# The modulation vectors of a two-layer diffusion step: from GpSimd and VectorE to TensorE and a later stage

## The chip, the cores and the metric

The kernel runs on one core of a Trainium2 chip, as one launch. A core has TensorE (PE, matrix products; PEld is its weight load), VectorE (DVE), ScalarE (ACT), GpSimd (POOL) and SyncE (SP, which here only issues DMAs). The metric is the device time of one execution in microseconds (us); less is better.

## The reference

The reference is one step of a backbone of two layers over 1152 tokens (1024 latent, 128 context) of width 1024. What matters here are the modulation vectors. Each layer has six of them for each of two conditions (`c` for latent tokens, `c_ctx` for context tokens):

```python
def ada_mod(cvec, w, b):
    m = jnp.matmul(jax.nn.silu(cvec), w) + b      # cvec (1024,), w (1024, 6144)
    return jnp.split(m, 6, axis=-1)
...
    sh1, sc1, g1, sh2, sc2, g2 = ada_mod(c_ctx, w_mod[l], b_mod[l])
    u = rms_norm(xp, norm1_g[l]) * (1.0 + sc1) + sh1
    mix, ... = context_mixer(u, lp, lam_init)
    xp = xp + g1 * mix
    xp = xp + g2 * swiglu(rms_norm(xp, norm2_g[l]) * (1.0 + sc2) + sh2, w_gate_up[l], w_down[l])
```

The mixers behind the input projection are a differential attention (4 heads), a gated delta rule and an mLSTM (4 heads each, two directions, in chunks). All is fp32.

## The kernel before, in words

Activations lie transposed, features on the 128 partitions, tokens along the rows, in three groups of 384 tokens (`GW`). A dense product is split in two fp32r parts (`split`, `load_w`), so a 128x128 block of weights by 384 tokens is three matrix products (`mm3`, L187, with the lines L189, L190 and L191). `load_w` (L174) loads 512 KB of raw weights into a slot `wr` (two slots, issued by ACT's queue), ACT casts it to `wh` (L183) and VectorE subtracts for `wl` (L184); there are three slots each of `wh` and `wl`.

A layer runs: `begin` (the first token-major columns), `w_in` (the input projection and what the mixers need), `mixers` (scans and attention with the output projection), the norm and `ffn`. In `w_in`, after the gates (`gates1`), a loop of ten blocks (`blk_b` six times, `blk_c` four times) makes 128 columns each: 72 products of 384 columns; `blk_b` follows with a short convolution on VectorE (L704 to L708) and, for four of them, sums of squares by small fp32 matrix products of 2 columns (L715, nine in the code of a block). Then come the preparation of nine chunks (`prep1`, L730), the inverses (`inverse`), `prep2`, and the attention's columns (`blk_a`, `tok_cols`). PSUM has eight banks: here two for `dn` and six for `pp`.

The modulation has 48 blocks of 128 values a layer. The first 16 of layer 1 are made at the start (`adaln`). The others are the side work of the ten-block loop, written out in `run` (L1359): blocks 16 to 47 of the layer, and in layer 1 also blocks 0 to 15 of layer 2. From the second turn on the loop adds up to six blocks (layer 1) or four (layer 2). A block (`ada`, L231) is one DMA of 512 KB by SP's queue into one of five slots `aw`, the weights transposed; for the first condition VectorE multiplies by the SiLU of the condition and sums along the row in one instruction (L240); for the second GpSimd multiplies (L243) and ACT sums (L244). The condition's SiLU, on all partitions, is `csb` (`ada_open`, L225). The pool of these tiles lies where the tiles of `prep1` come later.

In `ffn` (L354) a hidden block `gu` takes two weights and two rows of products (`pg`, `pu`), and `dn` takes two hidden blocks and their two down weights (`pd`), which `add_gated` (L344) adds to the residual on VectorE (L347). The loop issues `gu(j + 2)`, `dn((j, j + 1))`, `gu(j + 3)`.

A planner that simulates the engines sets the order of the instructions on each queue: of those that are ready in its own clock it takes the one that stands first in the program, and a tile gets a slot of its ring in the same way. On the chip each queue then runs strictly in that order.

Of the kernel before, what the change touches and what calls it, by code (L numbers as in the profile page):

```python
# [45 lines left out]
AWB = 5  # L46
# [6 lines left out]
HS = (0, 2, 1, 3)  # place of each head in the stored chunk matrices  # L53

# column ranges of the small parameter array
# [15 lines left out]
class Kern:  # L71
# [24 lines left out]
    # ---------------------------------------------------------------- constants  # L96
    def setup(self, es):
# [3 lines left out]
        # silu(c) for both conditions, split in two parts, as the stationary operand of the modulation product  # L101
# [18 lines left out]
    def setup2(self):  # L120
# [4 lines left out]
        # fp32r operands of the decay matrices: identity, ones, and a large negative number where masked  # L125
# [15 lines left out]
    def setup3(self):  # L141
        nc = self.nc
        # lambda of the attention and exp(A_log)
# [29 lines left out]
    # ---------------------------------------------------------------- dense products  # L173
# [32 lines left out]
    # ---------------------------------------------------------------- modulation vectors  # L206
    def adaln(self, l, jbs, pool, psp, tag, bufs, raw=None):
        """Blocks of 512 columns jbs of silu(c) @ w_mod + b_mod, as per-partition columns."""
# [16 lines left out]
    def ada_open(self, pool):  # L225
        """silu(c) for both conditions, on every partition."""
        self.csb = self.t(pool, [P, 2, D], "csb", 1)
        self.nc.sync.dma_start(self.csb, self.A["cB"].to_broadcast([P, 2, D]))
        self.nc.scalar.activation(self.csb, self.csb, AF.Silu)  # L229

    def ada(self, l, b, pool, bufs, dve):  # L231
        """Block b of silu(c) @ w_mod, a column per condition: products summed along the rows of the transposed weights."""
        nc = self.nc
        w = self.t(pool, [P, D], "aw", bufs)
        nc.sync.dma_start(w, self.A["w_mod1"][b] if l else self.A["w_mod0"][b - 16])
        for i in range(2):
            o = self.mod[l][:, b, i:i + 1]
            if i in dve:
                j = self.t(pool, [P, D], "aj", 1)
                nc.vector.scalar_tensor_tensor(out=j, in0=w, scalar=1.0, in1=self.csb[:, i], op0=ALU.mult, op1=ALU.mult, accum_out=o)  # L240
                continue
            p = self.t(pool, [P, D], "ap", APB)
            nc.gpsimd.tensor_tensor(out=p, in0=w, in1=self.csb[:, i], op=ALU.mult)  # L243
            nc.scalar.activation(p, p, AF.Copy, accum_out=o)  # L244
# [26 lines left out]
    # ---------------------------------------------------------------- norms  # L271
# [3 lines left out]
    def stat(self, g, k, xt):  # L275
        """Adds the squares of block k of group g to the group's sum."""
# [9 lines left out]
    def stats(self, g, x, pool):  # L286
        """The squares of group g, added up in two parts."""
# [9 lines left out]
    def rstd(self, g, psp, tag="st", bufs=2, tag2=None):  # L297
        """1/rms of the tokens of group g, on every partition, in PSUM."""
# [17 lines left out]
    def norm_g(self, x, a, sh, g, R):  # L316
        """A generator over the blocks of group g."""
# [17 lines left out]
    def norm_y(self, x, g, R):  # L335
        """The final norm of group g."""
        nc = self.nc
        for k in range(KB):
            t = self.t(self.nw, [P, GW], "nt", 4)
            nc.vector.scalar_tensor_tensor(out=t, in0=x[g][k], scalar=self.p(0, "fg")[:, k:k + 1], in1=R, op0=ALU.mult, op1=ALU.mult)  # L340
            nc.sync.dma_start(self.O["y"][:, k, GW * g:GW * g + GW], t)
            yield
# [7 lines left out]
    # ---------------------------------------------------------------- FFN  # L350
# [3 lines left out]
    def ffn(self, l, x, u, hp, psp, before, norm):  # L354
# [27 lines left out]
        def dn(bs):  # L382
# [6 lines left out]
            # the last one by groups, with the norm that follows  # L389
# [15 lines left out]
        gu(1)  # L405
        for j in range(0, HB, 2):
            if j + 2 < HB:
                gu(j + 2)
            dn((j, j + 1))
# [4 lines left out]
    # ---------------------------------------------------------------- input projection and preparation of the mixers  # L414
    def open_s(self, l):
        """Places in DRAM for what passes from the projection to the mixers, and the banks of the projection."""
# [20 lines left out]
    def begin(self, l, u, norm):  # L437
        """The first columns of the projection, along with the norm of the last group."""
        with self.pool("first", side="right") as pr:
# [3 lines left out]
            u[2] = list(norm(2, self.rstd(2, self.pp, "pp", 6)))  # L443
# [3 lines left out]
    def w_in(self, l, u, side, ed, pe):  # L447
        nc, A, S = self.nc, self.A, self.S
        with ExitStack() as es:
# [6 lines left out]
            side = list(side)  # L456
            with self.pool("side", side="right") as sp:
                self.ada_open(sp)
                n = -(-len(side) // (10 - LATE))
                for b in range(10):  # L460
# [6 lines left out]
                    if b >= LATE:  # L467
                        for l1, jb in side[:n]:
                            self.ada(l1, jb, sp, AWB, (0,))
                        side = side[n:]  # L470
                self.ada_bias(l, 16, 48)
                self.ada_scale(l, self.a2[l], "n2g", 32)
                if l == 0:
                    self.ada_bias(1, 0, 16)
                    self.ada_scale(1, self.a1[1], "n1g", 8)
# [30 lines left out]
    def tok_cols(self, l, u, i, pr):  # L506
        """Token-major columns: i = 0: cv and gates, 1, 2: av, 3: bg, 4: co."""
# [16 lines left out]
        for tt in range(NCH):  # L524
            g, j = divmod(tt, 3)
            cs = slice(128 * j, 128 * j + 128)
            ps = self.ps(self.pp, "pp", 6) if i == 0 and 1 < tt < 8 else self.ps(self.dn, "dn", 2)
# [995 lines left out]
```

## Time and profile before

| what | value |
|---|---|
| three runs | 3964.11, 3953.47, 3959.14 us; median 3959.14 |
| span of the profiled execution | 3963.4 us, first to last instruction |
| PE, PEld busy | 3587.5, 3417.7 us |
| VectorE, ScalarE, GpSimd busy | 2333.4, 1223.3, 904.9 us |
| mean granted TensorE clock | 0.939 of full speed |

The profile is of an execution of its own; its device time is not listed apart from its span, which lies within the three runs' times. "Busy" counts instructions on the engine, not its queue's waits. The granted clock has two levels, 1.00 (2.4 GHz) and 0.50 (1.2 GHz); a value between is a mean over a stretch. A matrix product's duration overlaps that of the next, so the pace is read from starts or from counts in a stretch. An fp32 product (not fp32r) stands as two instructions in the trace.

### The profile page before, as it was taken

The numbers are of one execution on the slowest core, as the hardware profiler recorded it, in microseconds if no ns is written. First come the engines' busy times: TensorE is split into PE (matmuls) and PEld (weight loads), VectorE is DVE, ScalarE is ACT, GpSimd is POOL, SyncE is SP. The second block draws the span as 40 slices with busy tenths as digits, with TensorE's granted clock in tenths as the row PEclk, the third lists the DMA queues.
The fourth block names the chain that finished last, engine by engine and source line by source line (L and its number), as shares of the span: only waits on it lengthen the run. The fifth ranks groups of instructions, "written<-read, shape, count | busy, mean of one in ns | idle before, by whom it ended". The sixth has DMA issues, their size and how long they took to land. (4 is left out here: it accounts for less than half of the span.)

```text
span 3963.4 us, 59219 instructions
## 1 busy us (share of the span) xinstructions
PE 3587.5 (91%) x22770; PEld 3417.7 (86%) x22770; DVE 2333.4 (59%) x5009; ACT 1223.3 (31%) x2544; POOL 904.9 (23%) x983
## 2 busy tenths in 40 slices
PE   7876888888899999999988798988889999999998
PEld 6876777788789999999987777878779999999997
DVE  7898575768654333333378957656785533433335
ACT  5343322535533111111143442233463411111111
POOL 2276340246310000000023735013551200000001
PEclk8988997899899999999998899979999999999999
DMA  5355743485411111111133575248652111111111
GB/s 206 129 197 165 241 159 111 118 242 155 149 54 38 38 49 43 38 43 43 40 121 135 192 246 182 90 114 246 175 160 68 38 43 38 44 47 38 38 49 59
DMA packets 270177, 434.11 MB, mean 110 GB/s; under 512 B 23880, under 2 KB 185736, under 8 KB 269640
## 3 DMA queue, kind: packets, MB, share of 16 engines
q1 hardware_dynamic: 240664, 324.28, 26.1%
q10 hardware_dynamic: 29232, 106.05, 8.4%
q8 instruction: 180, 2.95, 0.3%
q14 instruction: 101, 0.83, 0.1%
HBM read 315.85 MB, written 114.39 MB: 109 GB/s over the span
## 5 line engine op out<-in xcount | busy, mean ns | idle before, releaser
L347 DVE SCALAR_TENSOR_TENSOR x<-pd,mod,x 128x256 f32<-128x256 f32 (+1 forms) x832 | 404.1, 513 | 667.9 <-PE pd L191 667.2
L183 ACT CAST wh<-wr 128x1024 fp32r<-128x1024 f32 (+1 forms) x219 | 228.6, 1045 | 831.2 <-PE pu L190 457.6
L284 POOL TENSOR_TENSOR nacc<-nacc,nsq 128x384 f32<-128x384 f32 x48 | 52.0, 1083 | 1758.0 <-ACT nsq L283 1750.8
L189 PE MATMUL dn<-uh,wh 128*128 128x384 f32 x864 | 312.9, 362 | 82.7 <-ACT gw L726 37.7
L184 DVE TENSOR_TENSOR wl<-wr,wh 128x1024 fp32r<-128x1024 f32 (+1 forms) x219 | 279.9, 1287 | 164.1 <-ACT wh L183 163.6
L189 PE MATMUL pd<-hh,wh 128*128 128x384 f32 x1056 | 359.6, 341 | 6.9 <-DVE x L347 5.1
L190 PE MATMUL pg<-ul,wh 128*128 128x384 f32 x1056 | 357.9, 339 | 1.8 <-DVE ul L332 1.8
L189 PE MATMUL pg<-uh,wh 128*128 128x384 f32 x1056 | 356.0, 337 | 2.6 <-ACT uh L327 2.6
L190 PE MATMUL pd<-hl,wh 128*128 128x384 f32 x1056 | 356.2, 337 | 0.0
L191 PE MATMUL pd<-hh,wl 128*128 128x384 f32 x1056 | 355.9, 337 | 0.0
L189 PE MATMUL pu<-uh,wh 128*128 128x384 f32 x1056 | 355.3, 336 | 0.0
L190 PE MATMUL pu<-ul,wh 128*128 128x384 f32 x1056 | 355.3, 336 | 0.0
L191 PE MATMUL pg<-uh,wl 128*128 128x384 f32 x1056 | 353.1, 337 | 0.0
L191 PE MATMUL pu<-uh,wl 128*128 128x384 f32 x1056 | 349.1, 336 | 0.0
L190 PE MATMUL dn<-ul,wh 128*128 128x384 f32 x864 | 309.2, 358 | 0.0
L191 PE MATMUL dn<-uh,wl 128*128 128x384 f32 x864 | 307.8, 356 | 0.1
L243 POOL TENSOR_TENSOR ap<-aw,csb 128x1024 f32<-128x1024 f32 x80 | 253.2, 3191 | 220.9 <-ACT csb L229 147.0
L1232 PE MATMUL s<-K,Q 128*128 128x384 f32 (+1 forms) x800 | 229.1, 397 | 57.3 <-DMA Q<-QD 28.8
L189 PEld LDWEIGHTS dn<-uh,wh 128*128 128x128 f32 x864 | 175.1, 203 | 95.1 <-ACT gw L726 39.6
L1233 DVE TENSOR_SCALAR_CACHE_REDUCE e<-s 128x384 f32<-128x384 f32 (+1 forms) x400 | 209.8, 540 | 78.8 <-PE s L1232 73.2
L370 DVE TENSOR_TENSOR hs<-pu,hs 128x384 f32<-128x384 f32 x132 | 73.1, 554 | 239.8 <-PE pu L191 238.2
L189 PEld LDWEIGHTS pd<-hh,wh 128*128 128x128 f32 x1056 | 198.1, 188 | 15.8 <-issue 7.5
(354 smaller groups left out, 8650.3 us busy)
## 6 DMA issues: line engine op xcount, KB each, us to landing
wr<-in_w_gu_dram ACTq DMA_DIRECT2D x88, 512.0 KB
aw<-in_w_mod_dram SPq DMA_DIRECT2D x80, 512.0 KB
wr<-in_w_dn_dram ACTq DMA_DIRECT2D x44, 512.0 KB
wr<-in_w_st_dram ACTq DMA_DIRECT2D x36, 512.0 KB
rd<-RD SPq DMA_DIRECT2D x36, 512.0 KB
Q<-QD SPq DMA_DIRECT2D x64, 256.0 KB
RM<-em SPq DMA_DIRECT2D x36, 384.0 KB
rm<-RM SPq DMA_DIRECT2D x36, 384.0 KB
```

The costliest lines, as they stand in the source:

```text
L183: nc.scalar.copy(hi, r)
L184: (eng or nc.vector).tensor_tensor(out=lo, in0=r, in1=hi.bitcast(F32), op=ALU.subtract)
L189: mm(out, lhsT=wh, rhs=xh, start=start, stop=False)
L190: mm(out, lhsT=wh, rhs=xl, start=False, stop=False)
L191: mm(out, lhsT=wl, rhs=xh, start=False, stop=stop)
L243: nc.gpsimd.tensor_tensor(out=p, in0=w, in1=self.csb[:, i], op=ALU.mult)
L284: (nc.gpsimd if k in PST else nc.vector).tensor_tensor(out=self.acc[g], in0=self.acc[g], in1=s, op=ALU.add)
L347: nc.vector.scalar_tensor_tensor(out=x[g][k][:, lo:hi], in0=ps[:, lo:hi], scalar=gate[:, k, cnd:cnd + 1], in1=x[g][k][:, lo:hi], op0=ALU.m ...
L370: nc.vector.tensor_mul(s, pu[:, :GW], s)
L1232: nc.tensor.matmul(p[:, :w], lhsT=q[:, m, hl, 128 * j:128 * j + 128], rhs=K[m][:, 128 * ks[0]:128 * ks[0] + w], start=hl == 0, stop=hl == 1)
L1233: nc.vector.tensor_scalar(out=e[:, GW * i:GW * i + w], in0=p[:, :w], scalar1=0.125, scalar2=None, op0=ALU.mult, op1=ALU.max, accum_out=mx[ ...
```

## The change

Layer 1's blocks 16 to 47 become matrix products: the weights lie untransposed by blocks (`_blocks`), a block is eight fp32 products of 128x128 by the 2 columns of `cs`, all 32 blocks summing into one PSUM bank. The bank comes from `pp`, which has five instead of six everywhere. Layer 2's 48 blocks move into layer 1's `ffn`, five or six in each of nine turns, on VectorE alone, in three pieces of the row for each condition; the partial sums are added up once at j = 18. Their weights go into the two `wr` slots of the FFN's weights, loaded by SP's queue; the products' unused result goes into a bank of `st`; the SiLUs lie in free buffers of the norm's pool. GpSimd makes none. Layer 2's `w_in` has no side work. `tok_cols` uses `pp` for one token tile less; other edits take out comments.

```diff
-AWB = 5
+AWB = 4
+ACH = ((0, 384), (384, 768), (768, 1024))
...
+    def ada_pe(self, b, ps):
+        nc = self.nc
+        w = self.t(self.side, [P, D], "aw", AWB)
+        nc.sync.dma_start(w, self.A["w_mod0"][b - 16])
+        o = ps[:, 2 * (b - 16):2 * (b - 16) + 2]
+        for k in range(KB):
+            nc.tensor.matmul(o, lhsT=w[:, 128 * k:128 * k + 128], rhs=self.cs[:, k, :], start=k == 0, stop=k == KB - 1)
+
+    def ada_open(self):
+        nc = self.nc
+        self.apart = self.t(self.nw, [P, 48, 2, 3], "apart", 1)
+        self.csb = []
         for i in range(2):
+            for lo, hi in ACH:
+                t = self.t(self.nw, [P, GW], *(("nt", 4) if len(self.csb) < 4 else ("nacc", 3)))[:, :hi - lo]
+                nc.sync.dma_start(t, self.A["cB"][0, i:i + 1, lo:hi].to_broadcast([P, hi - lo]))
+                nc.scalar.activation(t, t, AF.Silu)
+                self.csb.append(t)
+
+    def ada(self, b, junk):
+        nc = self.nc
+        w = self.t(self.stage, [P, D], "wr", 2)
+        nc.sync.dma_start(w, self.A["w_mod1"][b])
+        for i in range(2):
+            for j, (lo, hi) in enumerate(ACH):
+                nc.vector.scalar_tensor_tensor(out=junk[:, :hi - lo], in0=w[:, lo:hi], scalar=1.0, in1=self.csb[3 * i + j],
+                                               op0=ALU.mult, op1=ALU.mult, accum_out=self.apart[:, b, i, j:j + 1])
+
+    def ada_close(self):
+        nc = self.nc
+        nc.vector.reduce_sum(self.mod[1].rearrange("p b i -> p (b i)"), self.apart.rearrange("p b i j -> p (b i) j"), axis=AX.X)
+        self.ada_bias(1, 0, 48)
+        self.ada_scale(1, self.a1[1], "n1g", 8)
+        self.ada_scale(1, self.a2[1], "n2g", 32)
...
         gu(1)
+        if l == 0:
+            self.ada_open()
+            junk = self.ps(psp, "st", 2)
         for j in range(0, HB, 2):
             if j + 2 < HB:
                 gu(j + 2)
+            if l == 0 and j < 20:
+                if j == 18:
+                    self.ada_close()
+                else:
+                    for b in range(16 * j // 6, 16 * (j + 2) // 6):
+                        self.ada(b, junk)
             dn((j, j + 1))
...
-            side = list(side)
-            with self.pool("side", side="right") as sp:
-                self.ada_open(sp)
-                n = -(-len(side) // (10 - LATE))
+            side = list(range(16, 48)) if l == 0 else []
+            with ExitStack() as ss:
+                if side:
+                    self.side = ss.enter_context(self.pool("side", side="right"))
+                    pm = self.ps(self.dn, "ad", 1)
...
-                    if b >= LATE:
-                        for l1, jb in side[:n]:
-                            self.ada(l1, jb, sp, AWB, (0,))
-                        side = side[n:]
-                self.ada_bias(l, 16, 48)
-                self.ada_scale(l, self.a2[l], "n2g", 32)
-                if l == 0:
-                    self.ada_bias(1, 0, 16)
-                    self.ada_scale(1, self.a1[1], "n1g", 8)
+                    for jb in side[4 * b:4 * b + 4]:
+                        self.ada_pe(jb, pm)
+                if side:
+                    m = self.mod[0][:, 16:48, :]
+                    nc.vector.tensor_add(m, pm[:, 0:64].rearrange("p (b i) -> p b i", i=2),
+                                         self.p(0, "bmod")[:, 16:48][:, :, None].to_broadcast([P, 32, 2]))
+                    self.ada_scale(0, self.a2[0], "n2g", 32)
...
-                ps = self.ps(pp, "pp", 6)
+                ps = self.ps(pp, "pp", 5)
...
-    out["w_mod0"] = x["w_mod"][0, :, 2048:].T.reshape(32, P, D)
+    out["w_mod0"] = _blocks(x["w_mod"][0, :, 2048:])
```

## Rows read from the trace of the kernel before

**Rows 1.** The profile's page, first part: busy time and share by engine.
```profile
PE 3587.5 (91%) x22770; PEld 3417.7 (86%) x22770; DVE 2333.4 (59%) x5009; ACT 1223.3 (31%) x2544; POOL 904.9 (23%) x983
```

**Rows 2.** Windows: stretch, length; PE, PEld, DVE, ACT, POOL busy (instructions); clock; DMA; GB/s.
```profile
2061.00:2264.00 203.00, 162.11 (x930) 157.70 (x930) 185.00 (x209) 82.79 (x135) 102.75 (x32) 0.87 0.47 157
...
1183.00:1933.00 750.00, 749.36 (x4306) 746.09 (x4305) 292.09 (x520) 136.07 (x222) 9.03 (x11) 1.00 0.13 41
```

**Rows 3.** Waits of PE in 2061:2264: total us, times, longest.
```profile
PE dn L189 <- ACT gw L726: 19.0, 2, 12.4
PE pp L715 <- ACT cv L712: 16.7, 1, 16.7
```

**Rows 4.** VectorE's timeline (start, length), and its line L240 in 90:375.
```profile
160.51 1.23 DVE L240 SCALAR_TENSOR_TENSOR aj<-aw,csb 128x1024 f32<-128x1024 f32 x1 [8.11 <-ACT csb L229]
...
161.78 3.30 DVE L240 SCALAR_TENSOR_TENSOR aj<-aw,csb 128x1024 f32<-128x1024 f32 x1
...
L240 DVE SCALAR_TENSOR_TENSOR aj<-aw,csb 128x1024 f32<-128x1024 f32 x48 | 114.0, 2374 | 9.0 <-ACT csb L229 8.1 <-DMA aw<-in_w_mod_dram 0.4
```

**Rows 5.** Windows of the tile `dn` alone (PE's count first), layers 1 and 2.
```profile
152.00:294.00 142.00, 93.91 (x479) 91.01 (x480) 0.00 (x0) 11.86 (x23) 0.82 0.60 198
2122.00:2264.00 142.00, 93.76 (x473) 91.38 (x474) 0.00 (x0) 11.88 (x23) 0.82 0.57 191
```

**Rows 6.** PE's timeline at L715, and two windows between.
```profile
148.11 4.08 PE L715 MATMUL pp<-con,cv 128*128 128x2 f32 x36
...
152.20:155.60 3.40, 3.40 (x12) 3.40 (x13) 0.18 (x1) 2.19 (x3) 0.00 (x0) 0.51 1.03 356
155.70:159.10 3.40, 3.40 (x27) 3.40 (x26) 0.00 (x0) 0.53 (x1) 0.00 (x0) 1.00 0.98 306
...
157.52 2.06 PE L715 MATMUL pp<-con,cv 128*128 128x2 f32 x18
...
200.84 4.00 PE L715 MATMUL pp<-con,cv 128*128 128x2 f32 x18 [16.73 <-ACT cv L712]
```

**Rows 7.** First chunk scores (L765) and first FFN products (`pg`): first and last start.
```profile
L765 PE MATMUL pp<-cv x72: 376/376/480, 382.2 to 536.4; 64*128 64x256 f32 x72
L765 PE MATMUL pp<-cv x72: 376/376/480, 2271.6 to 2417.7; 64*128 64x256 f32 x72
...
L189 PE MATMUL pg<-uh,wh x96: 332/336/522, 1178.1 to 1279.1; 128*128 128x384 f32 x96
...
L189 PE MATMUL pg<-uh,wh x94: 336/336/525, 3099.8 to 3197.7; 128*128 128x384 f32 x94
```

**Rows 8.** Groups by line: the attention's score evictions and their accumulator read.
```profile
L1233 DVE TENSOR_SCALAR_CACHE_REDUCE e<-s 128x384 f32<-128x384 f32 (+1 forms) x400 | 209.8, 540 | 78.8 <-PE s L1232 73.2 <-POOL e L1251 0.9 <-POOL z L1273 0.8
...
L1233 DVE DVE_READ_ACCUMULATOR e<-s 128x1 f32 x400 | 32.3, 81 | 0.0
```

**Rows 9.** Timelines of one FFN turn: weight loads, cast, subtract, first down product.
```profile
1528.45 0.33 ACTq L182 DMA_DIRECT2D wr<-in_w_dn_dram  x1
...
1541.14 0.34 ACTq L182 DMA_DIRECT2D wr<-in_w_dn_dram  x1
...
1555.45 1.05 ACT L183 CAST wh<-wr 128x1024 fp32r<-128x1024 f32 x1 [1.84 <-PE pg L190]
...
1556.54 1.23 DVE L184 TENSOR_TENSOR wl<-wr,wh 128x1024 fp32r<-128x1024 f32 x1 [2.33 <-ACT wh L183]
...
1559.59 0.34 PE L189 MATMUL pd<-hh,wh 128*128 128x384 f32 x1
```

**Rows 10.** Timelines: two loads of `aw`, and a product that waits for one.
```profile
344.30 0.49 SPq L235 DMA_DIRECT2D aw<-in_w_mod_dram  x1
...
346.02 0.56 SPq L235 DMA_DIRECT2D aw<-in_w_mod_dram  x1
...
348.63 1.23 DVE L240 SCALAR_TENSOR_TENSOR aj<-aw,csb 128x1024 f32<-128x1024 f32 x1 [0.35 <-DMA aw<-in_w_mod_dram]
```

**Rows 11.** Waits of PE in 2264:2430.
```profile
PE pp L775 <- DVE em L757: 5.5, 2, 3.7
```

More of the change, by code (lines that the diff above doesn't have):

```diff
@@ L223, in adaln @@
             self.ada_cols(l, jb, ps, 4, pool, psp, tag, bufs)
[L225 to L231, printed above, removed]
-        nc = self.nc
-        w = self.t(pool, [P, D], "aw", bufs)
-        nc.sync.dma_start(w, self.A["w_mod1"][b] if l else self.A["w_mod0"][b - 16])
-        for i in range(2):
[L237 to L244, printed above, removed]
+    def ada_pe(self, b, ps):
+        nc = self.nc
+        w = self.t(self.side, [P, D], "aw", AWB)
[3 more added lines that the diff above has]
+            nc.tensor.matmul(o, lhsT=w[:, 128 * k:128 * k + 128], rhs=self.cs[:, k, :], start=k == 0, stop=k == KB - 1)
@@ L442, in begin, with w_in @@
                 next(t)
-            u[2] = list(norm(2, self.rstd(2, self.pp, "pp", 6)))
+            u[2] = list(norm(2, self.rstd(2, self.pp, "pp", 5)))
             for _ in t:
                 pass
-    def w_in(self, l, u, side, ed, pe):
+    def w_in(self, l, u, ed, pe):
         nc, A, S = self.nc, self.A, self.S
@@ L526, in tok_cols @@
             cs = slice(128 * j, 128 * j + 128)
-            ps = self.ps(self.pp, "pp", 6) if i == 0 and 1 < tt < 8 else self.ps(self.dn, "dn", 2)
+            ps = self.ps(self.pp, "pp", 5) if i == 0 and 1 < tt < 7 else self.ps(self.dn, "dn", 2)
             o = ps[:, :wd]
@@ L621, in gates1 @@
         nc.vector.tensor_sub(lf, lf, m)
-        ps = self.ps(pp, "pp", 6)
+        ps = self.ps(pp, "pp", 5)
         for p in range(NCH):
@@ L630, in gates1 @@
         nc.vector.tensor_copy(Yb, Y[:, :, :, 4:8])
-        pb = self.ps(pp, "pp", 6)
+        pb = self.ps(pp, "pp", 5)
         nc.tensor.matmul(pb[:, :108], lhsT=self.rev, rhs=Yb.rearrange("p c a r -> p (c a r)"), start=True, stop=True)
@@ L647, in gates1 @@
         gg = GG
-        pe = self.ps(pp, "pp", 6)
+        pe = self.ps(pp, "pp", 5)
         for d in range(2):
@@ L660, in gates1 @@
         for q in range(3):
-            ps = self.ps(pp, "pp", 6)
+            ps = self.ps(pp, "pp", 5)
             for j in range(3):
@@ L712, in blk_b @@
             nc.scalar.activation(sq[:, :CVO], a, AF.Square)
-            ps = self.ps(self.pp, "pp", 6)
+            ps = self.ps(self.pp, "pp", 5)
             for c in range(NCH):
@@ L742, in prep1 @@
         hv = lambda a, w=64: a.rearrange("p (h v) -> p h v", h=H)
-        pt = self.ps(pp, "pp", 6)
+        pt = self.ps(pp, "pp", 5)
         for i in range(4):
@@ L750, in prep1 @@
         nc.sync.dma_start(S["VK"][c], vk)
-        pt = self.ps(pp, "pp", 6)
+        pt = self.ps(pp, "pp", 5)
         for i in range(2):
@@ L758, in prep1 @@
             em.append(e)
-        kk = [self.ps(pp, "pp", 6) for _ in range(2)]
-        cm = [self.ps(pp, "pp", 6) for _ in range(2)]
+        kk = [self.ps(pp, "pp", 5) for _ in range(2)]
+        cm = [self.ps(pp, "pp", 5) for _ in range(2)]
         for p in range(2):
@@ L773, in prep1 @@
             for x in range(2):
-                pd = self.ps(pp, "pp", 6)
+                pd = self.ps(pp, "pp", 5)
                 nc.tensor.matmul(pd, lhsT=self.idr, rhs=self.neg[d][:, None, :].to_broadcast([P, H, 128]), start=True, stop=False)
@@ L1337, in run @@
                 self.stats(0, x, bp)
-                Rs.append(self.rstd(0, self.pp, "pp", 6))
+                Rs.append(self.rstd(0, self.pp, "pp", 5))
                 self.pre = self.cvg_w(0, bp)
@@ L1343, in run @@
                     if g < 2:
-                        Rs.append(self.rstd(g, self.pp, "pp", 6))
+                        Rs.append(self.rstd(g, self.pp, "pp", 5))
                 self.setup3()
@@ L1358, in run @@
                 er.close()
-                self.w_in(l, u, [(l, b) for b in range(16, 48)] + [(1, b) for b in range(16) if l == 0], *ps)
+                self.w_in(l, u, *ps)
                 est.close()
```

## The prediction

> **What bounds the kernel now.** I read the busy table first: PE is busy 3587.5 of 3963.4 us [rows 1], so only what shortens TensorE's idle or half-clocked time can pay. The windows by stage come next [rows 2]. The first FFN (1183 to 1933) holds 4306 products in 750 us with PE busy 749.36 at clock 1.00: 0.174 us for a 384-column product, and nothing to win there. Layer 2's projection blocks (2061 to 2264) are the opposite: PE 162 of 203 us, VectorE 185, GpSimd 103, clock 0.87. PE's 41 idle us there are waits on ACT: 19.0 and 16.7 us are the two largest of the three lines [rows 3]. ACT itself stands behind VectorE, and the timeline of VectorE says why [rows 4]: of two `aj` products of 1024 elements, one behind the other at the start of GpSimd's work, the first took 1.23 us and the second 3.30; over 48 of them the mean is 2374 ns. So in both projections VectorE, slowed by GpSimd, sets the pace, and PE stalls behind it.
>
> **The change, part by part.**
>
> *Layer 2's projection loses its 32 blocks* (32 loads of 512 KB on SP's queue, 32 products and a `csb` load and SiLU less on each engine that had them). From 2122 to 2264 (142 us) PE did 473 matrix products [rows 5], 473 x 0.174 = 82 us, plus 36 short products of L715 at 0.114 us (2.06 us for 18, [rows 6]) = 4 us. So 142 - 86 = 56 us is the most that can go; if the stalls alone go, it is 41 us; if ACT is late for another reason, nothing. What is late next is the eviction chain of the blocks themselves: VectorE without 32 products of 2.4 us has 185 - 76 = 109 us at most, and less once its other operations have no GpSimd beside them, which is below PE's time. I take 44, leaving 12 us of waits. All that follows (chunk preparation, inverses, mixers) starts earlier by as much.
>
> *Layer 1's projection loses 48 blocks and gains 32 as matrix products.* Each block is 8 fp32 products of 128x128 by 2 columns. L715 is the same form and the trace has two instructions for one such product (18 for the nine of a block, [rows 6]), so 32 x 8 x 2 = 512 instructions: at 0.114 us 58 us, at the 0.222 us of the half clock (4.00 us for 18) 114 us [rows 6]. Which of the two is the question of this change. The trace shows both: after 4.08 us of nothing but such products the next stretch had a clock of 0.51 (half of 2.4 GHz, 12 products in 3.4 us); a run of 2.06 us between large products went with a clock of 1.00 [rows 6]. One block is 1.83 us, four (what one loop turn issues) 7.3 us. The weights can't be loaded before the gates' memory is free, about 152, when block 3 of 10 is under way, so at least 12 blocks are overdue and rank ahead of the projection's own products: about one every 2 to 3 us as the loads land. I expect the overdue ones mostly at 1.2 GHz and the later groups half and half: 58 + 38 = 96 us. The Trainium skill ("TensorE: Matmul & The Clock Gate", section "Why this matters for your kernels") puts clock drops in mid-kernel down to idle gaps between bursts of products; the row of 4.08 us shows a drop without an idle gap, so the trace differs. By that rule the sum would take 58 us, which is rival B.
>
> When chunk preparation can start: 152 + (479 x 0.174 = 83, [rows 5]) + 4 + 12 (waits as in layer 2) + 96 = 347, against 382.2 now [rows 7], where it waits for the last of layer 2's 16 extra blocks to leave the memory. But while it waits today, PE already does a part of the later products, so the rest of the layer is shorter than layer 2's: 1178.1 - 382.2 = 796 against 3099.8 - 2271.6 = 828 us [rows 7]. With 828 the FFN starts at 1175: 3 us gained. With 58 us it is 41 gained, with 114 and 8 us for large products caught at half clock, 23 lost.
>
> *Layer 2's 48 blocks on VectorE in the first FFN.* Three pieces (384, 384, 256) for each condition. Nearest row for 384: the score evictions with an accumulator, 540 ns, plus 81 to read it [rows 8]. From 540 at 384 and 1230 at 1024 [rows 4] a piece of 256 is some 400 ns. A block: 4 x 0.62 + 2 x 0.48 = 3.4 us, 48 of them 165 us; the least is two whole rows of 1.23 + 0.08, 2.6 us a block, and the most, if something like GpSimd's share slowed it, two of 3.3, 6.6. VectorE is busy 292 of 750 us [rows 2], so it has room, GpSimd being idle there, and the loads come at 0.13 DMA share. The cost is in the shared ring: the blocks take the two `wr` slots that the FFN's weights are loaded into, and in program order they come before the down-projection's two. In the loop shown [rows 9] a slot comes free at 1528.45, the second at 1541.14, and the second down weight was ready at 1557.77, 1.8 us before PE needed it at 1559.59. A load took between 2.6 (issue 346.02 to 348.63) and, if it was the one before, 4.3 us [rows 10]; I use 3. One slot: 6.4 us a block, two blocks by 1541. With two slots loads hide, so three more take 3 + 3 x 3.4 + about 3 us of VectorE's own work: 1557. Then the second down weight: 3 to load, 2.3 from cast to subtract (1555.45 to 1557.77): 1562.5, 3 us late. With six blocks (three of the nine loops) 6.4 us late. 6 x 3 + 3 x 6.4 = 37 us if nothing shifts, 0 if the schedule takes blocks while raw weights wait. The FFN's queues leave no row that decides; I take the middle, 18. With 4.3 for a load and 4 for a block (the rest of VectorE's work being in the way) only one block fits the single slot, four follow: 1541 + 4.3 + 16 + 3 = 1564, the weight ready 6.6 later at 1571, 11 us late; the prefetch gives back a part, and I put this end at 8 to 9 a loop, 78 in all. `ada_close` adds four small VectorE operations, `ada_open` six small loads and SiLUs, all before the end of the FFN and beside 25 us of products.
>
> *`pp` banks from 6 to 5* (the sixth holds the new products' sums). In layer 2's chunk preparation PE's only listed wait on this ring is 5.5 us [rows 11], the large products of `blk_a` filling the rest. Nothing at best, three such waits, 16 us, a layer at worst; I take 3 a layer, 6.
>
> **Sum.** -44 - 3 + 18 + 6 = -23 us of the span 3963.4. The three runs have a median of 3959.1, 4 below the span; the difference carries over: 3936.
>
> **Rivals.**
> A, the forecast above: 3936, its own range 3918 to 3956; chance 0.40.
> B, the products keep TensorE at 2.4 GHz, because the planner mixes them with large ones: layer 1 gains 41 instead of 3, 3959 - 44 - 41 + 18 + 6 = 3898. For it: the 2.06 us run without a drop. Against: the overdue dozen. 0.22.
> C, slower: in the FFN the weights are late in every loop because modulation tiles hold both `wr` slots and VectorE is queued with six pieces ahead of a subtract. Price 8 to 9 us a loop, 78 in all: 3959 - 44 - 3 + 78 + 6 = 3996. It decides from 6 us a loop on (53 us). For it: only 1.8 us of slack, PE busy 749 of 750 us. Against: VectorE is busy only 39% there. 0.18.
> D, the products run at 1.2 GHz throughout and drag the projection with them: layer 1 loses 23, 3959 - 44 + 23 + 18 + 6 = 3962, no change. For it: 200.84, where 18 took 4.00 us. 0.14.
> Others (the order in the mixers shifts, the bank costs 30): 0.06.
>
> **Numbers.** About 0.3% (12 us) is what a measurement of this kernel can tell from no change. Faster by more (under 3947): A 0.29, B 0.22, others 0.01 = 0.52. Within: A 0.11, C 0.02, D 0.08, others 0.02 = 0.23. Slower: C 0.16, D 0.06, others 0.03 = 0.25. The range 3888 to 4000 takes in B and C, and leaves out less than 2 in 10; since it holds both signs, A's own range stands above.
>
> **What will show it.** Right: in layer 2's projection VectorE's operations at 1.2 to 1.4 us, no PE wait of 12 to 17 us, and the first chunk's scores some 44 us nearer to the block start. The new products' line in layer 1: a mean start-to-start of 0.114 (B) or 0.22 us (D), and the clock in 152 to 350. In the FFN, PE's idle time before the down products, by loop: 0, 2 or 8 us. It would be wrong if PE still waited on ACT in layer 2 with GpSimd idle, or if the time went in the mixers, which the change doesn't touch.

## The result, and the profile after

The changed kernel took **4053.5 us** (median of four, 4045.74 to 4054.49) against 3959.8 before: ratio 1.0231, 95% interval 1.0217 to 1.0246, slower by 94 us where 3936 was forecast and 3888 to 4000 given as the range. The profiled execution is the fastest of the four (span 4043.9, time 4045.7), so the spans of the two profiled executions differ by 80.5 us and not by 94. Stages and windows below are of such single executions.

Lines moved with the edits: the chunk scores L765 are now L791, the decay products L775 and L776 are L801 and L802, the exponentials L779 are L805, L189 to L191 are L190 to L192. The page's first part [rows 1]:

```profile
PE 3672.4 (91%) x23282; PEld 3490.8 (86%) x23282; DVE 2235.4 (55%) x5425; ACT 1141.5 (28%) x2386; POOL 653.7 (16%) x903
```

PE's busy time grew by 85 us with 512 more products; that is no sum of their cost, since busy time changes with the clock as well: one of the 2-column products takes 0.222 us at half clock (1.2 GHz) and 0.114 at the full one [rows 6]. The stages tell more. Starts of the first `dn` product, of the first chunk scores, of the first `pg` product and of the last `pd` product, in us between them (the last column is the experiment told first below):

| stage | before | changed | six banks |
|---|---|---|---|
| layer 1: projection to first scores | 292.2 | 253.8 | 254.0 |
| layer 1: first scores to first FFN product | 795.9 | 879.0 | 833.4 |
| layer 1: FFN | 841.6 | 899.2 | 896.6 |
| layer 2: projection to first scores | 210.9 | 149.8 | 149.9 |
| layer 2: first scores to first FFN product | 828.2 | 869.6 | 827.0 |
| layer 2: FFN | 845.4 | 845.5 | 845.8 |

Both projections became shorter, by 38 and 61 us. Between the scores and the FFN 83 and 41 were lost, in code that the change touches by the number of `pp` banks and by one token tile that makes its columns in `dn` instead, and 58 in the first FFN. Of the 83, six banks give back 46; the other 37 go with the shorter projection: before, PE made 288 products of later columns more ahead of the first scores (1008 of 384 columns, now 720). In layer 2 six banks give back 43, all of it. Windows of the changed kernel (layer 2's projection, the first FFN, the stretch of layer 1 with the small products) and of the first FFN before:

```profile
2160.20:2310.00 149.80, 149.74 (x922) 146.87 (x920) 85.57 (x151) 45.81 (x70) 0.95 (x1) 0.98 0.31 98
1221.70:2121.00 899.30, 859.61 (x4776) 837.48 (x4777) 500.50 (x1208) 167.51 (x277) 28.27 (x34) 0.97 0.22 72
152.00:343.00 191.00, 191.00 (x1012) 190.75 (x1012) 34.02 (x44) 25.63 (x38) 0.95 (x1) 0.72 0.42 139
```

```profile
1178.10:2020.00 841.90, 835.84 (x4777) 828.47 (x4778) 347.12 (x629) 164.65 (x273) 28.35 (x34) 1.00 0.14 46
```

In layer 2's projection PE is busy 149.74 of 149.80 us; the waits for ACT [rows 3] are gone. The FFN runs the same 4777 products but for one; it has 33.6 us more of PE idle (39.7 against 6.1), and 23.8 more of busy time, at a mean clock of 0.97 instead of 1.00. So over this FFN 1 us of idle time came with 0.7 us of longer products.

The chunk scores, first and last start, in each layer [rows 7]:

```profile
L791 PE MATMUL pp<-cv x72: 376/376/480, 342.7 to 571.8; 64*128 64x256 f32 x72
L791 PE MATMUL pp<-cv x72: 376/376/480, 2310.0 to 2538.5; 64*128 64x256 f32 x72
```

They start 40 us earlier in layer 1 and end 35 later: 229 us for nine chunks instead of 154 and 146. One chunk shows why. First PE's decay products and two of ACT's rows of exponentials in the changed kernel (start, length), then the decay products of a chunk before:

```profile
345.85 0.49 PE L802 MATMUL pp<-gr,onr 2*128 2x512 f32 x1
351.38 0.49 PE L802 MATMUL pp<-gr,onr 2*128 2x512 f32 x1
356.90 0.49 PE L802 MATMUL pp<-gr,onr 2*128 2x512 f32 x1
362.43 0.49 PE L802 MATMUL pp<-gr,onr 2*128 2x512 f32 x1
```

```profile
346.44 1.14 ACT L805 ACTIVATE e<-pp,lrho 128x128 f32<-128x128 f32 x4 [2.51 <-PE pp L802]
351.90 1.15 ACT L805 ACTIVATE em<-pp,lrho 128x128 f32<-128x128 f32 x4 [1.80 <-PE pp L802]
```

```profile
2273.48 0.49 PE L776 MATMUL pp<-gr,onr 2*128 2x512 f32 x1
2275.21 0.50 PE L776 MATMUL pp<-gr,onr 2*128 2x512 f32 x1
2279.36 0.49 PE L776 MATMUL pp<-gr,onr 2*128 2x512 f32 x1
2281.24 0.50 PE L776 MATMUL pp<-gr,onr 2*128 2x512 f32 x1
```

In the code a chunk holds two banks of `kk` (the key scores) until its third decay product is used, and two of `cm` (the mLSTM's scores) until the fourth; of six banks two are left for the decay products, of five one. Before, they came in pairs 1.7 to 1.9 us apart, and four took 7.8 us here. Now the second needs the bank that the first one's exponentials empty (346.44 to 347.58). PE makes 27 large products between the two, up to 351, so the bank stands empty for some of that time; why the planner put so many there no run shows. The pace is one decay product every 5.5 us, four in 16.6. Over the nine chunks of a layer the mean from first to fourth is 16.2 us, and was 10.9 and 9.7; from the last score to the first decay product it is 4.8 and 4.6, and was 1.4. That makes most of the 10 us that a chunk's period grew (28 from 19.2 and 17.9). The Trainium skill ("Perfetto Trace Analysis", section "Matmuls") asks that independent groups of products rotate through different PSUM banks, so that one's eviction overlaps the next one's products; the trace agrees, with 5.5 us against 1.7.

From the chunks the delay reaches the FFN through the inverses. The first product behind them (`px`, L887) started 235 and 241 us after the first scores before, and starts 322 and 320 us after them now; with six banks it is 239 and 236. So it is late by some 80 us a layer, of which 46 and 43 reach the FFN, because PE makes later columns meanwhile. Those columns then run out: in layer 1 the last starts at 636.02. The next in PE's order is a score of the attention (L1258), which waits for its load of `Q` until 663.43, and `px` follows at 664.98. VectorE had finished the inverses at 645. A second wait stands at the other end, where the output projection needs the mixers' results (`ch`). With six banks `px` starts before the columns end. PE's two largest waits from the first scores to the first FFN product (total us, times, longest), in layers 1 and 2 of the changed kernel, and its waits for `Q` in layer 1 with six banks, where no wait for `ch` is listed:

```profile
PE s L1258 <- DMA Q<-QD: 41.6, 3, 27.1
PE pd L190 <- ACT ch L1320: 30.9, 1, 30.9
```

```profile
PE s L1258 <- DMA Q<-QD: 44.0, 3, 25.7
PE pd L190 <- ACT ch L1320: 27.1, 1, 27.1
```

```profile
PE s L1258 <- DMA Q<-QD: 10.9, 4, 5.9
```

In the first FFN the waits of PE are these, and one turn's ACT queue shows the cause:

```profile
PE pd L190 <- ACT wh L184: 22.9, 11, 2.7
PE pd L190 <- DVE x L365: 6.5, 11, 1.5
PE pg L190 <- ACT wh L184: 5.4, 8, 0.9
PE pd L192 <- DVE wl L185: 2.3, 8, 0.3
```

```profile
1456.16 0.33 ACTq L183 DMA_DIRECT2D wr<-in_w_dn_dram  x1
1459.61 1.05 ACT L184 CAST wh<-wr 128x1024 fp32r<-128x1024 f32 x1 [5.16 <-DVE st L254]
1460.13 0.34 ACTq L183 DMA_DIRECT2D wr<-in_w_dn_dram  x1
1460.56 0.51 ACT L203 CAST hh<-hs 128x384 fp32r<-128x384 f32 x1
1461.94 0.34 ACTq L183 DMA_DIRECT2D wr<-in_w_gu_dram  x1
1463.70 1.04 ACT L184 CAST wh<-wr 128x1024 fp32r<-128x1024 f32 x1 [2.63 <-DMA wr<-in_w_dn_dram]
```

Six modulation loads went out from 1426.19 on. The first down weight could be loaded only at 1456.16, when a slot came free, and the second at 1460.13; its cast waited 2.63 us for the load, and PE, idle for 2.68 and then 2.21 us, started its down products at 1460.71 and 1464.80. This turn loads six blocks. By turn, PE's gaps at the weights are none in the first, 2.3 to 2.6 us in the other five turns with five blocks and 5.4 us in the three with six, 29 us in all. The subtract (`wl`) is late by 2.3 us in all, the cast by 22.9. Windows around that stall (length, busy by engine, clock):

```profile
1460.70:1467.00 6.30, 3.79 (x12) 2.61 (x12) 2.90 (x3) 1.96 (x3) 0.00 (x0) 0.68 0.54 166
1467.00:1473.00 6.00, 5.54 (x26) 5.33 (x26) 2.28 (x3) 0.49 (x1) 0.00 (x0) 0.77 0.53 175
```

### The profile page after: what moved, and what is told of

The parts are those of the page before. It is cut to its first block, busy times and chain, and to the rows that moved or that the text cites. A ratio compares the mean times of both kernels' runs of the same rounds, so it can differ in the third digit from the quotient of the medians.

```text
span 4043.9 us, 60268 instructions
## 1 busy us (share of the span) xinstructions
PE 3672.4 (91%) x23282; PEld 3490.8 (86%) x23282; DVE 2235.4 (55%) x5425; ACT 1141.5 (28%) x2386; POOL 653.7 (16%) x903
## 4 chain that ended last, share of the span: by engine, by line
PE 68%; DMA 13%; DVE 12%; issue 2%; ACT 2%; SPq 1%; POOL 1%; POOLq 0%; DVEq 0%; ACTq 0%
PE pd L190 5%; PE pd L191 5%; PE pd L192 5%; PE dn L192 5%; PE dn L190 4%; PE dn L191 4%; PE pg L190 4%; PE pg L192 4%; PE pg L191 4%; PE pu L191 4%; PE pu L190 4%; PE pu L192 4%; PE s L1258 3%; DVE st L254 2%; PE ad L233 2%
## 5 line engine op out<-in xcount | busy, mean ns | idle before, releaser
L185 DVE TENSOR_TENSOR wl<-wr,wh 128x1024 fp32r<-128x1024 f32 (+1 forms) x219 | 267.9, 1229 | 330.1 <-ACT wh L184 329.3
L190 PE MATMUL pd<-hh,wh 128*128 128x384 f32 x1056 | 363.0, 344 | 32.8 <-ACT wh L184 22.9
L190 PE MATMUL pg<-uh,wh 128*128 128x384 f32 x1056 | 362.7, 343 | 8.8 <-ACT wh L184 5.4
L191 PE MATMUL pg<-ul,wh 128*128 128x384 f32 x1056 | 362.8, 344 | 1.2 <-DVE ul L350 1.2
L192 PE MATMUL pg<-uh,wl 128*128 128x384 f32 x1056 | 357.4, 342 | 0.6 <-DVE wl L185 0.6
L192 PE MATMUL pd<-hh,wl 128*128 128x384 f32 x1056 | 355.8, 340 | 2.3 <-DVE wl L185 2.3
L191 PE MATMUL pd<-hl,wh 128*128 128x384 f32 x1056 | 356.9, 338 | 0.0
L190 PE MATMUL pu<-uh,wh 128*128 128x384 f32 x1056 | 355.9, 337 | 0.0
L191 PE MATMUL pu<-ul,wh 128*128 128x384 f32 x1056 | 355.8, 337 | 0.0
L192 PE MATMUL pu<-uh,wl 128*128 128x384 f32 x1056 | 349.4, 337 | 0.0
L1258 PE MATMUL s<-K,Q 128*128 128x384 f32 (+1 forms) x800 | 223.4, 391 | 103.2 <-DMA Q<-QD 85.5
L190 PE MATMUL dn<-uh,wh 128*128 128x384 f32 x864 | 302.9, 351 | 0.1
L192 PE MATMUL dn<-uh,wl 128*128 128x384 f32 x864 | 302.3, 350 | 0.1
L191 PE MATMUL dn<-ul,wh 128*128 128x384 f32 x864 | 300.6, 348 | 0.0
L1258 PEld LDWEIGHTS s<-K,Q 128*128 128x128 f32 x800 | 138.4, 206 | 118.9 <-issue 76.9
L190 PEld LDWEIGHTS pd<-hh,wh 128*128 128x128 f32 x1056 | 199.0, 188 | 47.8 <-ACT wh L184 26.4
L190 PE MATMUL dn<-wh,uh 128*128 128x256 f32 (+1 forms) x640 | 191.7, 300 | 28.6 <-DVE gw L566 27.7
L190 PEld LDWEIGHTS pg<-uh,wh 128*128 128x128 f32 x1056 | 203.3, 193 | 12.4 <-ACT wh L184 8.9
```

The source lines that it names most:

```text
L185: (eng or nc.vector).tensor_tensor(out=lo, in0=r, in1=hi.bitcast(F32), op=ALU.subtract)
L190: mm(out, lhsT=wh, rhs=xh, start=start, stop=False)
L191: mm(out, lhsT=wh, rhs=xl, start=False, stop=False)
L192: mm(out, lhsT=wl, rhs=xh, start=False, stop=stop)
L1258: nc.tensor.matmul(p[:, :w], lhsT=q[:, m, hl, 128 * j:128 * j + 128], rhs=K[m][:, 128 * ks[0]:128 * ks[0] + w], start=hl == 0, stop=hl == 1)
```

## The experiments

| run | what it is | median us | ratio to before, 95% interval |
|---|---|---|---|
| e1_bank6 | changed, sums in a `pp` bank, six banks | 3956.5 | 1.0003, 0.9990 to 1.0017 |
| e2_five | before, five banks | 4111.6 | 1.0394, 1.0372 to 1.0416 |
| e3_noffn | changed, FFN blocks left out | 3995.9 | 1.0102, 1.0081 to 1.0123 |
| e4_own | changed, FFN blocks in a buffer of their own | 4065.1 | 1.0280, 1.0254 to 1.0307 |
| e6_spread | e1, FFN blocks one behind each weight | 3890.6 | 0.9836, 0.9815 to 0.9857 |
| e7_noad | e1, layer 1's products left out | 3855.2 | 0.9743, 0.9718 to 0.9769 |
| e8_deal | e1, layer 1's products dealt out | 3924.7 | 0.9921, 0.9889 to 0.9952 |
| e9_best | e6 and e8 | 3872.7 | 0.9792, 0.9763 to 0.9821 |
| e10_half | e9, half of layer 1's blocks on VectorE | 3838.6 | 0.9694, 0.9669 to 0.9719 |
| e11_allv | e9, all of them on VectorE | 3791.5 | 0.9577, 0.9556 to 0.9599 |

**The sixth bank** (e1_bank6).

```diff
-                    pm = self.ps(self.dn, "ad", 1)
+                    pm = self.ps(self.pp, "pp", 6)
...
-        ps = self.ps(pp, "pp", 5)
+        ps = self.ps(pp, "pp", 6)
...
```

The other edits put 6 for 5 in the same way; the token tile stays in `dn`, so it is not what cost the 97 us.

> The changed kernel with the products' sums in a bank of the `pp` ring, which has six again; all else as changed. Theory bank: four banks of the ring stay taken for a whole chunk (two of key scores, two of the mLSTM's), so with five one is left for the decay products and TensorE, ScalarE and TensorE again take turns; in the changed kernel nine chunks' scores span 229 and 228 us instead of 154 and 146. With six, layer 1 should go from its first chunk scores (343) to its FFN in 828 us, as layer 2 before, which puts the FFN at 1171 instead of 1222 (51 less), and layer 2 gains the 41 it lost: 4053 - 92 = 3961. Rival early: the chunks are slow because they now start before the projection's stores are done and share the DMA queues with it; then the bank does nothing: 4040 to 4055.

3956.5: 97 us come back (90 by the spans of the profiled executions). The scores in both layers, and the decay products of layer 1's first chunk:

```profile
L791 PE MATMUL pp<-cv x72: 376/376/480, 344.2 to 487.1; 64*128 64x256 f32 x72
L791 PE MATMUL pp<-cv x72: 376/376/480, 2263.5 to 2402.7; 64*128 64x256 f32 x72
```

```profile
346.16 0.49 PE L802 MATMUL pp<-gr,onr 2*128 2x512 f32 x1
347.89 0.50 PE L802 MATMUL pp<-gr,onr 2*128 2x512 f32 x1
352.04 0.49 PE L802 MATMUL pp<-gr,onr 2*128 2x512 f32 x1
353.93 0.50 PE L802 MATMUL pp<-gr,onr 2*128 2x512 f32 x1
```

143 and 139 us, although they start as early as in the changed kernel, and four decay products take 7.8 us again. The rival "early" falls.

**Five banks alone** (e2_five).

```diff
-        pt = self.ps(pp, "pp", 6)
+        pt = self.ps(pp, "pp", 5)
...
```

The other edits put 5 for 6 in the same way, and one token tile goes to `dn`.

> The kernel before with five `pp` banks instead of six (and the same token tile given to `dn`); nothing else changed, the sixth bank lies idle. Theory bank: layer 2 loses the 41 us of the changed kernel, layer 1 between 41 and 83: 4041 to 4083, and the scores of nine chunks span some 225 us in each layer. Rival early: within 12 us of 3959, scores still in about 150 us.

4111.6, slower by 156: the sign and the mechanism hold (scores over 224 and 230 us), the size is beyond the 124 that I allowed. From the first scores to the FFN layer 1 lost 90 us and layer 2 lost 52. PE here, as before, works on later products (82 us hold 244 of them, windows below) while the modulation blocks leave the memory. The token columns end at 623. Then PE waits 25.7 us for `Q`, as in the changed kernel, and makes attention products from 650 on; `px` starts only at 739.9, 116 us after the last decay product, where the other kernels need 71 to 85. VectorE's steps of the inverses take from 626.5 to 734.2, 108 us, where the other kernels need 52 to 72: in VectorE's queue 114 instructions of the attention stand between them (43.6 us), and at the first of these VectorE stops for 22.02 us, until PE has its scores. So the additional loss goes with this order of the queue. How much of the 90 us it makes was not separated.

```profile
300.00:382.00 82.00, 52.33 (x244) 50.74 (x244) 72.77 (x65) 29.68 (x56) 56.31 (x28) 0.81 0.50 159
382.00:623.00 241.00, 219.12 (x1412) 190.33 (x1412) 111.75 (x211) 64.33 (x182) 50.89 (x88) 0.94 0.52 176
623.00:746.00 123.00, 70.97 (x342) 53.45 (x341) 99.62 (x318) 41.89 (x100) 55.27 (x90) 0.72 0.32 81
```

```profile
PE s L1232 <- DMA Q<-QD: 25.7, 1, 25.7
```

```profile
651.09 0.56 DVE L1233 TENSOR_SCALAR_CACHE_REDUCE e<-s 128x384 f32<-128x384 f32 x1 [22.02 <-PE s L1232]
```

**The FFN without the blocks** (e3_noffn).

```diff
-                    for b in range(16 * j // 6, 16 * (j + 2) // 6):
-                        self.ada(b, junk)
+                    if j == 0:
+                        nc.vector.memset(self.apart, 0.0)
```

> The changed kernel with the loads and products of layer 2's 48 blocks left out of the first FFN (layer 2's modulation is then its bias alone); sums, SiLUs and closing operations stay. From the first to the last products the first FFN took 842 us before and 899 changed. If these blocks are the whole loss there: 4053 - 57 = 3996, no PE waits of 2 to 5 us before the down products. Rival, that the loss is in part the FFN's own (u products late, a colder clock at its start): 10 to 30 us come back, 4025 to 4043.

3995.9, as expected; the FFN takes 840.5 us. The blocks are the whole loss there.

**A buffer of their own** (e4_own).

```diff
-        w = self.t(self.stage, [P, D], "wr", 2)
-        nc.sync.dma_start(w, self.A["w_mod1"][b])
...
+        for j, (lo, hi) in enumerate(ACH):
+            w = self.t(pool, [P, GW], "am", 1)[:, :hi - lo]
+            nc.sync.dma_start(w, self.A["w_mod1"][b, :, lo:hi])
```

> The changed kernel with layer 2's blocks loaded in three pieces into a buffer of their own of 384 columns (all the memory that is left) instead of the two `wr` slots; the same 288 VectorE products. Theory ring: weights are late because modulation tiles hold both `wr` slots until VectorE is through with them, so with the ring untouched 45 to 57 us come back: 3996 to 4008. Rival VectorE: weights are late because their subtract stands in VectorE's queue behind the pieces, and a piece that waits for its load now stops the subtract too: little comes back, 4035 to 4075.

4065.1, in the rival's range: nothing came back, the FFN takes 908 us. But the wait is another one. PE's waits in that FFN, and VectorE's:

```profile
PE pd L190 <- DVE x L365: 37.6, 23, 4.1
...
PE pd L190 <- ACT wh L184: 1.5, 1, 1.5
```

```profile
DVE st L254 <- DMA am<-in_w_mod_dram: 230.2, 132, 4.2
```

The late weights are gone (22.9 to 1.5 us), so in the changed kernel the weights were late because of the ring. In their place 132 pieces wait on VectorE for a load that a single small buffer cannot hide, and the residual adds behind them keep the `pd` banks. Both theories of this run were half right; it does not say what the ring alone is worth.

**One block behind each weight** (e6_spread).

```diff
+        next(self.mods, None)
         return hi, lo
...
+    def blocks(self, junk):
+        for b in range(48):
+            self.ada(b, junk)
+            yield
+        self.ada_close()
+        yield
```

> The kernel of e1_bank6 (3956 us, 55 of them lost in the first FFN) with layer 2's blocks dealt out one behind each weight load of that FFN, through the same two `wr` slots, instead of five or six at a time ahead of the down weights. Theory ring: it is the bunch that holds both slots; a single block holds one slot for its load and its products (about 3 + 3.7 us) of the 12.5 us that a weight lasts, so the next weight still comes in time: 40 to 55 come back, 3901 to 3916, PE's waits for the ACT cast go from 23 us to under 3. Rival VectorE: as with the buffer of its own, pieces that wait for their load stop VectorE's queue and the residual adds behind it: 3935 to 3965, with PE waiting for the residual add.

3890.6, 66 less than e1_bank6 and 10 better than the best that I had named (the profiled executions differ by 55). The first FFN takes 846.7 us instead of 896.6, with the same 288 products in the same two slots; the rest is 7 more behind layer 1's scores and 14 less behind layer 2's, for which no run shows a cause. PE's largest wait in that FFN, and what is left of the one for the cast:

```profile
PE pd L191 <- DVE x L366: 5.8, 10, 1.5
...
PE pg L191 <- ACT wh L184: 0.4, 1, 0.4
```

So it was the bunch ahead of the down weights, not the sharing and not VectorE's load: VectorE is as busy (501 us) as in the changed kernel. The bunch leaves the slots and VectorE's queue at once here; that the slots mattered and not the queue ahead of the subtract is read from the changed kernel's waits, 22.9 us for the cast and 2.3 for the subtract.

**The price of layer 1's products** (e7_noad; the products and loads are left out).

```diff
-                    for jb in side[4 * b:4 * b + 4]:
-                        self.ada_pe(jb, pm)
+                    if side and b == 0:
+                        nc.vector.memset(pm[:, 0:64], 0.0)
```

> The kernel of e1_bank6 with the loads and the 512 small products of layer 1's 32 blocks left out (those modulation columns are then their bias). Theory: the products cost TensorE the 95 us that their line was busy, most of it at 1.2 GHz, and nothing hides them: first chunk scores of layer 1 at 344 - 95 = 249, total 3956 - 95 = 3861. Rival: the scores come earlier but the chunks then wait for VectorE and their DMAs, and part is given back: 3880 to 3920. Rival clock: the drop to 1.2 GHz slows large products too, 105 to 125 come back: 3831 to 3851.

3855.2 (median of two): 101 us less, between the theory and the rival of the clock. From the projection to the scores 149.8 us instead of 254.0, so 104 for the 32 blocks: 92 of the line itself, and 12 that fit large products caught at half clock. From 152 to 238 the granted clock is 0.97 without the small products and 0.63 with them (e1_bank6), PE being busy all 86 us in both.

**Dealt out** (e8_deal).

```diff
+    def deal1(self, b, g):
+        if b >= 2:
+            for _ in range(2 if g == 2 else 1):
+                next(self.deal, lambda: None)()
```

> The kernel of e1_bank6 with layer 1's 32 blocks dealt out one or two behind each 24 large products from block 2 of the projection on, instead of four behind each 72. If runs of one or two blocks (1.8 to 3.7 us) leave TensorE at 2.4 GHz, the products cost 512 x 0.114 = 58 instead of 95: 3919, clock of 152 to 343 at 0.95 or above. If the clock falls all the same, 3945 to 3965, clock still 0.72 to 0.80.

3924.7, 32 less, though the clock of 0.95 that I named wasn't reached. The line, and windows:

```profile
L233 PE MATMUL pp<-cs,aw x512: 165/252/355, 162.8 to 323.8; 128*128 128x2 f32 x171
```

```profile
152.00:200.00 48.00, 48.00 (x231) 48.00 (x232) 11.92 (x24) 9.62 (x13) 0.00 (x0) 0.57 0.51 169
200.00:250.00 50.00, 50.00 (x327) 50.00 (x325) 18.06 (x17) 8.95 (x14) 0.00 (x0) 0.93 0.42 143
250.00:300.00 50.00, 50.00 (x315) 50.00 (x314) 2.51 (x3) 6.51 (x10) 0.00 (x0) 0.90 0.52 176
300.00:332.00 32.00, 32.00 (x193) 31.80 (x192) 3.88 (x7) 3.55 (x6) 0.95 (x1) 0.84 0.32 112
```

The mixture keeps 0.90 and more from 200 to 300 and 0.84 in the last stretch; before 200 the overdue blocks come as their loads land, and the clock is 0.57. The line's busy time is 70 us instead of 92, the projection got 14 us shorter, and 26 products of later columns (4.5 us) now stand ahead of the scores. Of the rest of the gain 11 us lie between layer 1's scores and its FFN, and no run shows their cause; the five times spread from 3908.9 to 3936.9. Idle time does not account for the 0.57: PE was busy all 48.00 of those 48 us. The Trainium skill ("TensorE: Matmul & The Clock Gate", section "Why this matters for your kernels") names idle gaps as the cause of such drops; the trace differs here as it did at the 4.08 us of [rows 6].

**Together, and layer 1's blocks on VectorE** (e9_best, e10_half, e11_allv).

```diff
+    def ada_v(self, b, cb):
+        w = self.t(self.side, [P, D], "aw", AWB)
+        nc.sync.dma_start(w, self.A["w_mod0"][b - 16])
+        for i in range(2):
+            j = self.t(self.side, [P, D], "aj", 1)
+            nc.vector.scalar_tensor_tensor(out=j, in0=w, scalar=1.0, in1=cb[:, i], op0=ALU.mult, op1=ALU.mult,
+                                           accum_out=self.mod[0][:, b, i:i + 1])
...
+                    self.deal = iter([lambda jb=jb: self.ada_v(jb, cb) for jb in side])
```

> The kernel of e6_spread (3891 us) with layer 1's products dealt out as in e8_deal. If the two gains add: 3891 - 14 (what e8_deal saved from the first block to the first scores) to 3891 - 32 (what its time saved), 3859 to 3877. If e8_deal's further gain was only another order in the mixers, 3877 or above.

> The kernel of e9_best with every other one of layer 1's 32 blocks (16) on VectorE alone, as whole rows with the condition's SiLU on all partitions, dealt out between the 16 on TensorE. Theory: without GpSimd beside it VectorE's product takes 1.23 us, so 32 of them are 39 us of an engine that was busy 34 of the 192 us, and they hide; TensorE's 16 blocks cost half of the 104 us that 32 cost in e1_bank6 or less: layer 1's first scores at 270 to 290 instead of 344, total 3810 to 3840. Rival: VectorE in program order makes the convolutions and evictions late as in the kernel before, with PE waits for ACT or VectorE of 10 us and more: 3850 to 3880.

> As e10_half with all 32 blocks on VectorE and none on TensorE. If VectorE at 1.23 us a product still hides them (79 us in the 90 us or so that are left of the ten blocks once the memory is free), first scores of layer 1 at 240 to 255 and 3785 to 3800; if VectorE sets the pace, 152 + 79 + some 50 of its own work = 281 or later, with clear PE waits: 3820 to 3870. If the kernel before was slow for VectorE's count of products and not for GpSimd beside it, near 3890.

3872.7, 3838.6 and 3791.5: e9's time is what the two gains make together, as far as its spread (3865.9 to 3882.8) tells: the other theory, another order in the mixers, began at 3877. Moving 16 blocks and then all 32 from TensorE to VectorE pays each time (e10 within its range of time, with the scores at 288). With all 32 on VectorE the scores start at 308, so VectorE does set the pace there (busy 131 of 140 us from 160 to 300), and PE still waits little (its largest wait is the last line below):

```profile
L242 DVE SCALAR_TENSOR_TENSOR aj<-aw,cb x64: 1202/1220/2034, 160.9 to 299.7; 128x1024 f32<-128x1024 f32 x64
```

```profile
PE dn L191 <- ACT gw L985: 4.6, 3, 3.0
```

PE fills that time with later columns, 1044 products of 384 columns ahead of the first scores where e7_noad has 720: its first FFN product starts at 1073.6, as in e7_noad, which has no such blocks at all (1074.0). The two signs that I had named for e11 disagree: the first scores at 308 are those of the branch in which VectorE sets the pace (281 or later), the time, 47 us below e10's, is that of the branch in which it hides the work. The median of a product is 1.22 us where it was 3.24 with GpSimd beside it. e11_allv beats the kernel before by 4.2% and the changed one by 6.5%.

## Why the prediction was wrong, point by point

- **`pp` banks from 6 to 5: forecast +6, bound 32; measured 97** (changed against e1_bank6; 90 by spans, 46 and 43 of it between scores and FFN). This step failed, and it alone carries the sign: without it the rest sums to about -4. I priced it by PE's waits on the ring [rows 11], which are small because PE has other products to take. But the chunks' end releases the inverses, and these the mixers; a longer turn between PE and ACT delays that chain whether or not PE idles meanwhile. After the change `px` comes some 80 us later behind the first scores in each layer; PE's later columns hide about half, and the rest shows as waits of 26 to 27 us for `Q` and 27 to 31 us for `ch`, one of each a layer. The code would have told that the ring is short: four of the banks are held through most of a chunk.
- **The FFN's ring: forecast +18 between 0 and 78; measured 55 to 58** (the FFN's length, and e3_noffn). The mechanism was the one worked out in that term: two slots held, the down weights late by 3 us in a turn of five blocks and 6.4 in one of six, 37 in all. Measured were 2.3 to 2.6 (none in the first turn) and 5.4, 29 in all. What failed was to halve the 37, and to leave out the half clock behind each stall, 24 of the 58. By its size, 6.4 us a turn, the loss is just above the 6 from which I had rival C decide, and below its 8 to 9. Of C's two causes, the held slots are what PE waited for; the pieces ahead of the subtract cost 2.3 us against the cast's 22.9.
- **Layer 2's projection: forecast -44, at most -56; measured -61.** Right in kind: VectorE's pace and PE's waits for ACT are gone. The bound ended at 2264, 7.6 us ahead of the first scores, and it had the number of products fixed. PE made 54 products of later columns more ahead of the scores before (774 of 384 columns, 720 now), some 9 us; with the 41 us of idle time, and some 11 us from a clock of 0.98 instead of 0.88 over the stage, that is 61.
- **Layer 1's products: forecast -3; measured about 0** (292.2 + 795.9 before, 254.0 + 833.4 in e1_bank6). Most of the working held: 96 us for 512 instructions against the 95 us that the line was busy, and the 828 us that follow once PE has no later products done ahead against 833. That the scores came at 342.7 where the sum said 347 is partly luck: the 12 us of waits in it did not come (PE is busy throughout from 152 to 343), and 12 us of large products at half clock, which only rival D had, did. Rival B (2.4 GHz) and D (1.2 GHz throughout) are both out: the clock was mixed. That the same blocks could cost nothing on VectorE alone was not among the rivals.
- **The sum of what was measured**: -61 + 0 + 57 + 97 = 93, against 94 by the medians. The first three are from single executions and the last from medians; by spans alone the bank is 90 and the sum 86 against 80.5, so that 93 comes so close is partly chance.

## What to carry to other kernels

Count the banks that a stage holds from start to end before you take one from its ring: what is left is the depth of its pipeline, and the wait table of the busiest engine didn't show that depth here, since PE filled its waits with other work until this ran out. Deal side work out one item per step; the same loads and operations in bunches held two slots long enough to stop the main stream. And ask why an engine was slow before moving its work: here VectorE was slow because of GpSimd beside it, and with GpSimd out of the way it took all 80 blocks for some 6 us: 48 of them cost the first FFN that much (846.7 against 840.5 without them), and the other 32 left its start where it is without them (1073.6 against 1074.0).

## What I had not expected of the hardware

Short stalls in a run of products, 2 to 5 us a turn and none longer than 2.7 us, came with 0.7 times as much again in longer products at a lower clock: 33.6 us of idle time and 23.8 us of longer products in the first FFN. In e4_own the ratio is 0.4 (47 us of additional idle time, 19 of additional busy time). And the small products pull the clock down with PE busy throughout and large ones between them: 0.57 over 48 us in e8_deal, 0.72 over 191 us in the changed kernel, and 0.97 from 152 to 238 in e7_noad, which has none of the 512.
